# A decoder block in fp32 on one core: the order of the first stage's loads, table loads and bank hand-over

## The chip, the cores and the metric

The kernel runs on one core of one Trainium2 chip. The metric is device time in microseconds (us) of that core for one execution. A core has TensorE (PE: matmuls, its weight loads shown as PEld), VectorE (DVE), ScalarE (ACT), GpSimd (POOL) and SyncE (SP), whose queue issues all of this kernel's transfers.

## The reference, cut to what matters

One layer, batch 1, 512 tokens (T), width 2048 (D), everything fp32. The vector c sets shift, scale and gate of both sub-layers (adaLN).

```python
c_act = jax.nn.silu(c)
mod = c_act @ w_ada[l] + b_ada[l]
sh1, sc1, gt1, sh2, sc2, gt2 = jnp.split(mod[:, None, :], N_MOD, axis=-1)
h = _rmsnorm(x, norm1_g[l]) * (1.0 + sc1) + sh1
p = h @ w_in[l]
y_rwkv = _rwkv7_mixer(p[..., :N_RWKV_COLS], ...)
y_pool = _pool_mixer(p[..., N_RWKV_COLS:], pool_w[l], pool_b[l], pool_scale[l])
mix = jnp.concatenate([y_rwkv, y_pool], axis=-1) @ w_out[l]
x = x + gt1 * mix
h = _rmsnorm(x, norm2_g[l]) * (1.0 + sc2) + sh2
x = x + gt2 * _conv_ffn(h, w_up[l], conv_w[l], conv_b[l], w_down[l])
return _rmsnorm(x, norm_f_g)
```

## The kernel before, in words

The block is kept transposed: 128 channels on the partitions, 512 tokens along the row; x is 16 tiles of 128x512 (k = 0 to 15), loaded two at a time. A product of fp32 matrices is made of three (`mm3`, lines 112 to 114): each operand is cut into a hi part (fp32r) and a lo part, and PE adds hi x hi, lo x hi and hi x lo in one bank. `split_weights` does that for weights: a load of 256 KB to `wraw` (4 buffers), a cast on ScalarE to `whi` (line 106, 3 buffers), a subtraction on VectorE to `wlo` (line 108, 3 buffers). A pair `whi`, `wlo` serves 4 x 3 products.

**The first stage** makes modulated activations and, with them, the first eight tiles of the input projection.

1. Constants are loaded: `vec`, `cmat`, then the tables `masks`, `mlev`, `lanei` and `prec` (lines 69 to 78), which only the mixer and the pool read.
2. c is loaded to every partition (`cb`, line 171, 1 MB) and put through Silu on ScalarE (line 172); its first row is stored to `cact` in DRAM, from where the mixer's later adaLN work reads it again as `cq`.
3. x is loaded. ScalarE squares its tiles (`sq`, two buffers, line 188), VectorE adds them up in `sacc` (line 189, 15 adds, each on the one before).
4. `rms_stats` sums over the partitions on PE (`pst`), `rms_rows` takes the root on ScalarE (line 152, with a load of the table of functions) and the reciprocal on VectorE, makes four diagonal tiles (`rdiag`, line 156), and `rms_bcast` multiplies them on PE by ones (`psb`), so that each partition holds the row of 1/rms. ScalarE copies it (`rs`, line 193).
5. The loop over k: two rows of `mod` come from two adaLN products on VectorE (line 204; a tile `wa` of 1 MB, 128x2048, against `cb`, with the sum along the row; parts 1 and 0 are scale and shift). Then `gsc` (line 206), the shift's bias (line 208), and `modulate`: `h` on VectorE (line 139), the hi part `ah` on ScalarE (line 140), the lo part `al` on VectorE (line 141). Two weight tiles of 512 columns are split, and 8 x 3 products go into the eight banks `pf[0]` to `pf[7]`.

**The joint.** All eight banks are read out. `shift` (lines 225 and 226) is a scaled copy on ScalarE and a shifted multiply-add on VectorE: `xwa`, `xg1`, `xg2` from the first three banks, with Tanh and two Sigmoids behind them, then r, k, v of the first pair of heads; the last two banks are copied to `upad` (line 257) for the pooling. Then the pool of banks `ps0` is closed, and `psa` takes the same banks for the mixer. Its first tile in the order of work is a projection tile `mm`, 48 products (16 k x 3).

**The second stage** is the mixer: `win_pair(p)` projects three tiles for pair p, shifts and stores them; `start_pair`, `stage_b` and `stage_c` are a pair's chain of decays, triangular inverses and states, with many short steps on PE, VectorE and ScalarE. `pool_front` and `pool_back` make one group of the pooling (windowed sums on VectorE, line 275; two by two products on PE, line 290). `ada_rest` spreads 192 further adaLN products (`jkr`, line 343, 128x512) over the pairs.

A scheduler sets the order on each engine from the order of the program and from priorities: what stands in `with hp():` goes ahead of other work that is ready. On an engine instructions then run in that order, each waiting for what it reads. SP issues the transfers one by one, in its order; a transfer also waits for the one eight before it. `reuse_waits` says what a tile of a new pool waits for: by default for all readers of the space that the pool takes over, with "tile" for those of the tile's own space.

```python
pool_back(3, pool_front(3), load_pw(3))
with hp():
    q = start_pair(0)
    stage_b(0, q)
win_pair(1)
for p in range(NP):
    if p + 1 < NP:
        if p + 2 < NP:
            win_pair(p + 2)
        with hp():
            qn = start_pair(p + 1)
```

Of the kernel before, what the change touches and what calls it, by code (L numbers as in the profile page):

```python
# [9 lines left out]
F32 = mybir.dt.float32  # L10
# [44 lines left out]
def block_kernel(ctx, tc, a, out, stop=None, dbg=None):  # L55
# [13 lines left out]
    nc.sync.dma_start(masks, a["mask4"][:, :, :])  # L69
    mlev = cp.tile([P, 2, 64], F32, tag="mlev", name="mlev")  # L70
    nc.sync.dma_start(mlev, a["mlev"][:, :, :])
# [4 lines left out]
    nc.sync.dma_start(lanei, a["lanei"][:, :, :])  # L76
    prec = cp.tile([P, 16], F32, tag="prec", name="prec")
    nc.sync.dma_start(prec, a["prec"][:, :])
# [90 lines left out]
    if True:  # L169
        cb = p0.tile([P, D], F32, tag="cb", name="cb")  # L170
        nc.sync.dma_start(cb, a["c"][0:1, :].partition_broadcast(P))
        S.activation(cb, cb, AF.Silu)
        nc.sync.dma_start(cact, cb[0:1, :])
        xs = []
        for i in range(8):
            xt = p0.tile([P, 2, T], F32, tag=f"x{i}", name=f"x{i}")
            nc.sync.dma_start(xt, a["xT"][:, 2 * i : 2 * i + 2, :])
            xs += [xt[:, 0, :], xt[:, 1, :]]
        rstd = p0.tile([P, T], F32, tag="rs0", name="rs0")
        with tc.tile_pool(name="ps00", bufs=1, space=PSUM) as ps00:  # L180
            pst = ps00.tile([P, NC], F32, tag="st", name="pst")
            acc = p0.tile([P, T], F32, tag="sacc", name="sacc")
            for k in range(KT):
                if k == 0:
                    S.activation(acc, xs[k], AF.Square)
                    continue
                sq = p0.tile([P, T], F32, tag="sq", name="sq", bufs=2)
                S.activation(sq, xs[k], AF.Square)
                V.tensor_add(acc, acc, sq)
            rms_stats(pst, acc)  # L190
            psb = ps00.tile([P, T], F32, tag="bc", name="psb")
            rms_bcast(psb, rms_rows(p0, pst, NC), NC)
            S.copy(rstd, psb)
# [4 lines left out]
        for k in range(KT):  # L198
            for part in (1, 0):
                j = part * 16 + k  # L200
                wa = p0.tile([P, D], F32, tag="wa", name="wa", bufs=4)
                nc.sync.dma_start(wa, a["ada1"][j, :, :])
                jk = p0.tile([P, D], BF16, tag="jk", name="jk", bufs=1)
                V.scalar_tensor_tensor(jk, wa, 1.0, cb, op0=ALU.mult, op1=ALU.mult,
                                       accum_out=mod[:, j : j + 1])
# [6 lines left out]
            H.append((hi, lo))  # L212
            for i0 in range(0, 8, WC // P):
                wh, wl = split_weights(a["win0"][k, :, i0 * P : i0 * P + WC])
                for ii in range(WC // P):
                    sl = slice(ii * P, (ii + 1) * P)
                    mm3(pf[i0 + ii], wh[:, sl], wl[:, sl], *H[k], start=k == 0, stop=k == KT - 1)
# [5 lines left out]
        if True:  # L223
            def shift(ps, m, dst):
                S.activation(dst, ps, AF.Copy, scale=drv[:, m : m + 1])
                V.scalar_tensor_tensor(dst[:, 1:T], ps[:, 0 : T - 1], col("mu", m), dst[:, 1:T],
                                       op0=ALU.mult, op1=ALU.add)
# [8 lines left out]
            shift(pf[0], 24, xwa)  # L236
            S.activation(xwa[0:64, :], xwa[0:64, :], AF.Tanh)
            xg1 = ra.tile([P, T], F32, tag="xg1", name="xg1")
            shift(pf[1], 25, xg1)
            S.activation(xg1, xg1, AF.Sigmoid)  # L240
            xg2 = ra.tile([P, T], F32, tag="xg2", name="xg2")
            shift(pf[2], 26, xg2)
            S.activation(xg2, xg2, AF.Sigmoid)
# [14 lines left out]
            ps0ctx.close()  # L258

# [40 lines left out]
    psa = psctx.enter_context(tc.tile_pool(name="psa", bufs=1, space=PSUM))  # L300
# [320 lines left out]
    pool_back(3, pool_front(3), load_pw(3))  # L621
    with hp():
        q = start_pair(0)
        stage_b(0, q)
    win_pair(1)
# [358 lines left out]
```

## Time and profile before

| | |
|---|---|
| three runs | 2449.73, 2451.7, 2455.32 us; median 2451.7 |
| profiled execution | 2452.14 us; span from the first to the last instruction 2450.0 us; mean granted clock of TensorE 0.992 |
| PE busy | 2347.1 us (96% of the span), 13714 products |
| VectorE busy | 1408.7 us (57%) |
| ScalarE busy | 874.6 us (36%) |
| GpSimd busy | 23.7 us (1%) |
| transfers | 352.61 MB, mean 144 GB/s |

How to read it: times in the rows are counted from the start of the span. Busy shares are means over stages that differ; the stretches of rows 1 below tell them apart. In a row of the timeline the first number is the start, the second the time from the first start to the last end, "x8" says how many instructions stand together, and the bracket gives the idle time of the engine ahead of them and what ended it. The clock in a stretch is the granted one, 1.00 being 2.4 GHz.

### The profile page before, as it was taken

Reading aid. Unit: us, or ns where it says so; the run is one execution under the profiler, and the core shown is the slowest. Engines: PE = TensorE matmul, PEld = TensorE weight load, DVE = VectorE, ACT = ScalarE, POOL = GpSimd, SP = SyncE. Lnnn points to the kernel's source line nnn. Section 1 sums busy time; section 2 is a strip of 40 time slices with the busy share of each in tenths; the row PEclk is TensorE's granted clock in tenths of the full one; section 3 lists DMA queues with packets and bytes.
Section 4 is the critical chain, followed back from the end, with each engine's and each line's share of the span. In section 5 each row is a group of like instructions: output and inputs, shape, how many; then the busy total and the mean of one; then the engine's idle time right before and its main releaser. Section 6 shows DMA issues by size and latency. Waiting matters only on the chain.

```text
span 2450.0 us, 36089 instructions
## 1 busy us (share of the span) xinstructions
PE 2347.1 (96%) x13714; PEld 1872.0 (76%) x13714; DVE 1408.7 (57%) x2698; ACT 874.6 (36%) x1402; POOL 23.7 (1%) x29
## 2 busy tenths in 40 slices
PE   4889999999999999999999999999999999999997
PEld 3656666667667889887888888888888888888887
DVE  7987677787774357757534443444344434444457
ACT  3244443443433336532223322333233323323333
POOL 0000000000000002100000000000000000000000
PEclk9999999999999999999999999999999999999999
DMA  9975564556662635538533333333332333332335
GB/s 353 337 233 152 166 185 140 163 162 178 169 200 85 203 111 185 181 113 260 161 96 98 96 98 95 99 96 98 95 99 95 99 95 99 95 99 95 99 97 174
DMA packets 232160, 352.61 MB, mean 144 GB/s; under 512 B 74865, under 2 KB 80177, under 8 KB 227761
## 3 DMA queue, kind: packets, MB, share of 16 engines
q1 hardware_dynamic: 231986, 350.30, 46.0%
q8 instruction: 107, 1.75, 0.3%
q14 instruction: 67, 0.55, 0.1%
HBM read 334.22 MB, written 16.00 MB: 143 GB/s over the span
## 4 chain that ended last, share of the span: by engine, by line
PE 68%; DMA 3%; DVE 2%; ACT 1%; issue 0%; SPq 0%; POOL 0%; DVEq 0%; ACTq 0%; POOLq 0%
PE b L112 20%; PE b L114 20%; PE b L113 20%; DMA wraw<-wup 1%; PE mm L112 1%; PE mm L113 1%; PE mm L114 1%; DMA war<-ada 0%; PE pa L290 0%; DMA slot<-ada 0%; DMA wraw<-wdn 0%; DVE wlo L108 0%; DVE x L863 0%; PE pa L114 0%; PE pa L113 0%
## 5 line engine op out<-in xcount | busy, mean ns | idle before, releaser
L108 DVE TENSOR_TENSOR wlo<-wraw,whi 128x512 fp32r<-128x512 f32 x772 | 533.2, 692 | 694.9 <-ACT whi L106 679.6
L106 ACT CAST whi<-wraw 128x512 fp32r<-128x512 f32 x788 | 489.3, 622 | 1229.0 <-PE b L113 925.2
L114 PE MATMUL b<-hh,wlo 128*128 128x512 f32 (+1 forms) x1472 | 561.2, 381 | 5.9 <-DVE wlo L108 5.0
L112 PE MATMUL b<-hh,whi 128*128 128x512 f32 (+1 forms) x1472 | 560.0, 380 | 0.0
L113 PE MATMUL b<-hl,whi 128*128 128x512 f32 (+1 forms) x1472 | 559.5, 380 | 0.0
L112 PE MATMUL b<-ah,whi 128*128 128x512 f32 (+1 forms) x992 | 353.4, 357 | 4.3 <-ACT whi L106 2.5
L114 PE MATMUL b<-ah,wlo 128*128 128x512 f32 (+1 forms) x992 | 351.9, 355 | 0.8 <-DVE wlo L108 0.8
L113 PE MATMUL b<-al,whi 128*128 128x512 f32 (+1 forms) x992 | 352.1, 355 | 0.0
L114 PEld LDWEIGHTS b<-hh,wlo 128*128 128x128 f32 x1472 | 277.0, 188 | 62.1 <-DVE wlo L108 8.5
L112 PEld LDWEIGHTS b<-hh,whi 128*128 128x128 f32 x1472 | 276.9, 188 | 52.9 <-ACT whi L106 0.5
L113 PEld LDWEIGHTS b<-hl,whi 128*128 128x128 f32 x1472 | 277.0, 188 | 52.3
L112 PEld LDWEIGHTS b<-ah,whi 128*128 128x128 f32 x992 | 187.5, 189 | 33.7 <-ACT whi L106 4.3
L113 PEld LDWEIGHTS b<-al,whi 128*128 128x128 f32 x992 | 187.6, 189 | 27.4 <-DVE al L134 1.1
L114 PEld LDWEIGHTS b<-ah,wlo 128*128 128x128 f32 x992 | 187.6, 189 | 26.8 <-DVE wlo L108 1.2
L112 PE MATMUL mm<-ah,whi 128*128 128x512 f32 x464 | 192.4, 415 | 6.3 <-ACT upad L257 5.5
L113 PE MATMUL mm<-al,whi 128*128 128x512 f32 x464 | 191.8, 413 | 0.0
L114 PE MATMUL mm<-ah,wlo 128*128 128x512 f32 x464 | 190.1, 410 | 0.0
L343 DVE SCALAR_TENSOR_TENSOR jkr<-war,cq 128x512 bf16<-128x512 f32 x192 | 131.3, 684 | 18.7 <-DMA war<-ada 15.9
L848 DVE SCALAR_TENSOR_TENSOR x<-b,mod,x 128x512 f32<-128x512 f32 x80 | 59.7, 750 | 111.4 <-PE b L114 111.3
L112 PEld LDWEIGHTS mm<-ah,whi 128*128 128x128 f32 x464 | 88.4, 190 | 35.1 <-issue 10.4
L113 PEld LDWEIGHTS mm<-al,whi 128*128 128x128 f32 x464 | 88.3, 190 | 29.3 <-issue 13.0
L114 PEld LDWEIGHTS mm<-ah,wlo 128*128 128x128 f32 x464 | 88.4, 191 | 23.8 <-issue 6.3
(259 smaller groups left out, 2282.0 us busy)
## 6 DMA issues: line engine op xcount, KB each, us to landing
wraw<-wup SPq DMA_DIRECT2D x368, 256.0 KB, 3.0
war<-ada SPq DMA_DIRECT2D x192, 256.0 KB, 3.4
wraw<-wdn SPq DMA_DIRECT2D x192, 256.0 KB, 2.7
wraw<-win SPq DMA_DIRECT2D x140, 256.0 KB, 4.0
wa<-ada SPq DMA_DIRECT2D x32, 1024.0 KB, 6.9
wraw<-wout SPq DMA_DIRECT2D x88, 256.0 KB, 3.0
slot<-ada SPq DMA_DIRECT2D x64, 256.0 KB, 3.7
sp<-spill SPq DMA_DIRECT2D x21, 256.0 KB, 2.7
```

The costliest lines, as they stand in the source:

```text
L106: S.copy(hi, raw)
L108: eng.tensor_tensor(lo, raw, hi[:, :].bitcast(F32), op=ALU.subtract)
L112: PE.matmul(ps, wh, xh, start=start, stop=False)
L113: PE.matmul(ps, wh, xl, start=False, stop=False)
L114: return PE.matmul(ps, wl, xh, start=False, stop=stop)
L343: V.scalar_tensor_tensor(jk, wa, 1.0, cq[0], op0=ALU.mult, op1=ALU.mult, accum_out=modq[:, kq, j : j + 1])
L848: V.scalar_tensor_tensor(x2[f], ps, mod[:, 80 + f : 81 + f], x2[f], op0=ALU.mult, op1=ALU.add)
```

## The change

It has these parts:

- The loads of the four tables leave the constants' place and stand in the loop at k = 8, behind `modulate`.
- Two adaLN tiles (k = 0, scale and shift) are loaded ahead of x and multiplied ahead of the squares; the loop makes no adaLN product at k = 0.
- A root of one column (`warm`) stands in the program behind Silu.
- The store of `cact` moves behind the loads of x. The squares have four buffers instead of two.
- Tanh and the Sigmoids stand behind all six shifts and both copies. The pool `psa` has `reuse_waits="tile"`.
- The projection of pair 1 stands ahead of the pool's last group and of pair 0 in the program, and that group is inside `hp()`.

The diff, cut to its core:

```diff
@@ constants
-    nc.sync.dma_start(masks, a["mask4"][:, :, :])
-    nc.sync.dma_start(mlev, a["mlev"][:, :, :])
-    nc.sync.dma_start(lanei, a["lanei"][:, :, :])
-    nc.sync.dma_start(prec, a["prec"][:, :])
+    def load_tables():
+        nc.sync.dma_start(masks, a["mask4"][:, :, :])
+        nc.sync.dma_start(mlev, a["mlev"][:, :, :])
+        nc.sync.dma_start(lanei, a["lanei"][:, :, :])
+        nc.sync.dma_start(prec, a["prec"][:, :])
@@ first stage
+        def load_ada(k, part):
+            wa = p0.tile([P, D], F32, tag="wa", name="wa", bufs=4)
+            nc.sync.dma_start(wa, a["ada1"][part * 16 + k, :, :])
+            return wa
+
+        def ada(k, part, wa):
+            j = part * 16 + k
+            jk = p0.tile([P, D], BF16, tag="jk", name="jk", bufs=1)
+            V.scalar_tensor_tensor(jk, wa, 1.0, cb, op0=ALU.mult, op1=ALU.mult, accum_out=mod[:, j : j + 1])
+
         cb = p0.tile([P, D], F32, tag="cb", name="cb")
         nc.sync.dma_start(cb, a["c"][0:1, :].partition_broadcast(P))
         S.activation(cb, cb, AF.Silu)
-        nc.sync.dma_start(cact, cb[0:1, :])
+        warm = p0.tile([P, 1], F32, tag="warm", name="warm")
+        S.activation(warm, eps[:, 0:1], AF.Sqrt)
+        early = [load_ada(0, 1), load_ada(0, 0)]
+        ada(0, 1, early[0])
+        ada(0, 0, early[1])
...
+        nc.sync.dma_start(cact, cb[0:1, :])
...
-                sq = p0.tile([P, T], F32, tag="sq", name="sq", bufs=2)
+                sq = p0.tile([P, T], F32, tag="sq", name="sq", bufs=4)
...
         for k in range(KT):
-            for part in (1, 0):
-                j = part * 16 + k
-                wa = p0.tile([P, D], F32, tag="wa", name="wa", bufs=4)
-                nc.sync.dma_start(wa, a["ada1"][j, :, :])
-                jk = p0.tile([P, D], BF16, tag="jk", name="jk", bufs=1)
-                V.scalar_tensor_tensor(jk, wa, 1.0, cb, op0=ALU.mult, op1=ALU.mult,
-                                       accum_out=mod[:, j : j + 1])
+            if k:
+                for part in (1, 0):
+                    ada(k, part, load_ada(k, part))
...
             H.append((hi, lo))
+            if k == 8:
+                load_tables()
@@ out of the banks
-            shift(pf[0], 24, xwa)
-            S.activation(xwa[0:64, :], xwa[0:64, :], AF.Tanh)
...
-            shift(pf[1], 25, xg1)
-            S.activation(xg1, xg1, AF.Sigmoid)
...
-            shift(pf[2], 26, xg2)
-            S.activation(xg2, xg2, AF.Sigmoid)
+            for i, t in enumerate((xwa, xg1, xg2)):
+                shift(pf[i], 24 + i, t)
...
             ps0ctx.close()
+            S.activation(xwa[0:64, :], xwa[0:64, :], AF.Tanh)
+            S.activation(xg1, xg1, AF.Sigmoid)
+            S.activation(xg2, xg2, AF.Sigmoid)
...
-    psa = psctx.enter_context(tc.tile_pool(name="psa", bufs=1, space=PSUM))
+    psa = psctx.enter_context(tc.tile_pool(name="psa", bufs=1, space=PSUM, reuse_waits="tile"))
@@ second stage
-    pool_back(3, pool_front(3), load_pw(3))
+    win_pair(1)
     with hp():
+        pool_back(3, pool_front(3), load_pw(3))
         q = start_pair(0)
         stage_b(0, q)
-    win_pair(1)
```

The order in three places. The names carry numbers of buffers where a name has several.

**VectorE, from the start to the first `h`**, before:

```order
L100 TENSOR_SCALAR b1p<-vec 128x16
L189 TENSOR_TENSOR sacc<-sacc,sq 128x512 x15
L204 SCALAR_TENSOR_TENSOR jk,mod<-wa,cb 128x2048
L153 RECIPROCAL rstd<-rstd 128x4
L206 SCALAR_TENSOR_TENSOR gsc_88<-mod,b1p,vec 128x1
L156 TENSOR_SCALAR rdiag<-cmat,rstd 128x128 x4
L204 SCALAR_TENSOR_TENSOR jk,mod<-wa,cb 128x2048
L108 TENSOR_TENSOR wlo<-wraw,whi 128x512
L208 TENSOR_TENSOR mod<-mod,vec 128x1
L108 TENSOR_TENSOR wlo<-wraw,whi 128x512
L139 SCALAR_TENSOR_TENSOR h<-x_118,gsc_88,rs_134 128x512
```

and now:

```order
L102 TENSOR_SCALAR b1p<-vec 128x16
L180 SCALAR_TENSOR_TENSOR jk,mod<-wa,cb 128x2048
L221 SCALAR_TENSOR_TENSOR gsc_84<-mod,b1p,vec 128x1
L180 SCALAR_TENSOR_TENSOR jk,mod<-wa,cb 128x2048
L223 TENSOR_TENSOR mod<-mod,vec 128x1
L208 TENSOR_TENSOR sacc<-sacc,sq 128x512 x15
L155 RECIPROCAL rstd<-rstd 128x4
L158 TENSOR_SCALAR rdiag<-cmat,rstd 128x128 x4
L110 TENSOR_TENSOR wlo<-wraw,whi 128x512 x2
L141 SCALAR_TENSOR_TENSOR h<-x_123,gsc_84,rs_140 128x512
```

The two adaLN products (`jk`) have gone from behind the sums and from between `rdiag` and the weight split to ahead of all sums, with what follows them (`gsc`, the addition to `mod`).

**ScalarE, from the last squares to the root**, with the semaphores that each waits for, before:

```order
L188 ACTIVATE sq<-x_130 128x512 [waits DMAHW6_49,DVE_49]
L188 ACTIVATE sq<-x_130 128x512 [waits DVE_49]
L188 ACTIVATE sq<-x_132 128x512 [waits DMAHW7_49,DVE_49]
L188 ACTIVATE sq<-x_132 128x512 [waits DVE_49]
L152 ACT_TABLE_LOAD [waits PE_49]
L152 ACTIVATE rstd<-pst,eps 128x4 [waits Pool_49]
```

and now, first the beginning and then the same place:

```order
L188 ACT_TABLE_LOAD
L188 ACTIVATE warm<-eps 128x1 [waits Pool_49]
L185 ACT_TABLE_LOAD
L185 ACTIVATE cb<-cb 128x2048 [waits DMAHW2_49]
L204 ACTIVATE sacc<-x_123 128x512 [waits DMAHW5_49]
```

```order
L207 ACTIVATE sq<-x_135 128x512 [waits DMAHW3_49,DVE_49]
L207 ACTIVATE sq<-x_135 128x512 [waits DVE_49]
L207 ACTIVATE sq<-x_137 128x512 [waits DMAHW4_49,DVE_49]
L207 ACTIVATE sq<-x_137 128x512 [waits DVE_49]
L154 ACT_TABLE_LOAD
L154 ACTIVATE rstd<-pst,eps 128x4 [waits PE_49]
```

The new root `warm` has come out ahead of Silu, with a table load each, and a table load stands ahead of the root of the sums as before. The wait for PE has moved from that load to the root behind it.

**The joint, on ScalarE**, from the third shift to the weight casts, before:

```order
L225 ACTIVATE xg_1057<-pf_207,drv 128x512
L237 ACT_TABLE_LOAD
L237 ACTIVATE xwa<-xwa 64x512
L240 ACT_TABLE_LOAD
L240 ACTIVATE xg_1053<-xg_1053 128x512
L243 ACTIVATE xg_1057<-xg_1057 128x512
L225 ACTIVATE rkv<-pf_208,drv 128x512
L225 ACTIVATE rkv<-pf_209,drv 128x512
L225 ACTIVATE v<-pf_210,drv 128x512
L257 COPY upad<-pf_211 128x512
L257 COPY upad<-pf_212 128x512
L106 CAST whi<-wraw 128x512 x6
```

and now:

```order
L242 ACTIVATE xg_1053<-pf_213,drv 128x512
L242 ACTIVATE rkv<-pf_214,drv 128x512
L242 ACTIVATE rkv<-pf_215,drv 128x512
L242 ACTIVATE v<-pf_216,drv 128x512
L270 COPY upad<-pf_217 128x512
L272 ACT_TABLE_LOAD
L272 ACTIVATE xwa<-xwa 64x512
L270 COPY upad<-pf_218 128x512
L273 ACT_TABLE_LOAD
L273 ACTIVATE xg_1052<-xg_1052 128x512
L274 ACTIVATE xg_1053<-xg_1053 128x512
L108 CAST whi<-wraw 128x512 x5
```

**The joint, on VectorE**, from the last shift on, before:

```order
L226 SCALAR_TENSOR_TENSOR v<-pf_210,vec,v 128x511
L275 TENSOR_TENSOR sw<-upad 128x527
L108 TENSOR_TENSOR wlo<-wraw,whi 128x512
L275 TENSOR_TENSOR sw<-sw 128x525
L108 TENSOR_TENSOR wlo<-wraw,whi 128x512
L275 TENSOR_TENSOR sw<-sw 128x521
L343 SCALAR_TENSOR_TENSOR jkr,modq<-war,cq 128x512
L275 TENSOR_TENSOR sw<-sw 128x513
```

and now:

```order
L243 SCALAR_TENSOR_TENSOR v<-pf_216,vec,v 128x511
L269 MEMSET upad 128x16 x2
L291 TENSOR_TENSOR sw<-upad 128x527
L291 TENSOR_TENSOR sw<-sw 128x525
L291 TENSOR_TENSOR sw<-sw 128x521
L291 TENSOR_TENSOR sw<-sw 128x513
L359 SCALAR_TENSOR_TENSOR jkr,modq<-war,cq 128x512
L296 SCALAR_TENSOR_TENSOR z<-sw,upad 128x512
L291 TENSOR_TENSOR sw<-upad 128x527
L297 TENSOR_TENSOR z<-sw,prec 128x16
L110 TENSOR_TENSOR wlo<-wraw,whi 128x512
```

On ScalarE the functions and their table loads have moved behind the six shifts (Tanh stands ahead of the second copy, not behind it), and the casts stand behind all of them in both; on VectorE the first weight split (`wlo`) has moved from behind one sum of the pool to behind five, an adaLN product (`jkr`) and the first two `z`.

## Rows read from the trace of the kernel before

**Rows 1.** Stretches: start:end us, length; busy us (count); PEclk; DMA share; GB/s

```profile
0.00:10.00 10.00, 0.00 (x0) 0.00 (x0) 0.41 (x4) 1.28 (x1) 0.90 (x9) 1.00 0.77 260
10.00:14.00 4.00, 0.00 (x0) 0.00 (x0) 0.44 (x1) 3.42 (x4) 0.00 (x0) 1.00 1.01 384
30.00:150.00 120.00, 94.95 (x362) 72.10 (x362) 115.78 (x160) 30.04 (x49) 0.00 (x0) 0.96 0.88 319
161.00:166.50 5.50, 5.07 (x12) 4.03 (x13) 5.50 (x12) 1.35 (x3) 0.00 (x0) 0.50 0.53 179
200.00:700.00 500.00, 483.73 (x4655) 333.25 (x4655) 378.83 (x1010) 212.54 (x323) 0.00 (x0) 1.00 0.58 168
```

**Rows 2.** Waits of VectorE, 30 to 150 us: us in total, times, longest

```profile
DVE al L141 <- ACT ah L140: 2.5, 13, 0.2
DVE wlo L108 <- ACT whi L106: 0.7, 1, 0.7
```

**Rows 3.** Timeline of VectorE, the sums to the first modulate

```profile
19.59 6.26 DVE L189 TENSOR_TENSOR sacc<-sacc,sq 128x512 f32<-128x512 f32 x8 [0.55 <-ACT sq L188]
25.77 2.29 DVE L204 SCALAR_TENSOR_TENSOR jk<-wa,cb 128x2048 bf16<-128x2048 f32 x1
...
33.94 0.74 DVE L139 SCALAR_TENSOR_TENSOR h<-x,gsc,rs 128x512 f32<-128x512 f32 x1
```

**Rows 4.** Timeline of PE at the joint

```profile
155.56 0.39 PE L114 MATMUL pf<-ah,wlo 128*128 128x512 f32 x1
161.44 0.76 PE L112 MATMUL mm<-ah,whi 128*128 128x512 f32 x1 [5.48 <-ACT upad L257]
...
166.60 0.39 PE L112 MATMUL mm<-ah,whi 128*128 128x512 f32 x1
...
175.08 1.10 PE L290 MATMUL pa<-z,pw 128*128 128x512 f32 x2
```

**Rows 5.** Timeline of SP's queue, the first issues

```profile
1.66 0.42 SPq L69 DMA_DIRECT2D masks<-mask  x1
...
3.85 0.43 SPq L171 DMA_DIRECT2D cb<-c  x1
```

**Rows 6.** Transfers issued from 0 to 60 us: count, KB each, median us to landing

```profile
wa<-ada SPq DMA_DIRECT2D x12, 1024.0 KB, 7.4
...
cb<-c SPq DMA_DIRECT2D x1, 1024.0 KB, 6.7
cmat<-cmat SPq DMA_DIRECT2D x1, 320.0 KB, 3.3
vec<-vec SPq DMA_DIRECT2D x1, 297.5 KB, 3.0
```

**Rows 7.** Timeline of ScalarE, the norm's root and the copy of its rows

```profile
27.86 1.28 ACT L152 ACT_TABLE_LOAD   x1 [2.93 <-PE pst L147]
29.15 0.26 ACT L152 ACTIVATE rstd<-pst,eps 128x4 f32<-128x4 f32 x1
...
32.70 0.59 ACT L193 COPY rs<-psb 128x512 f32<-128x512 f32 x1 [2.26 <-PE psb L160]
```

**Rows 8.** Timeline of ScalarE, the hi part of an activation late in the loop

```profile
141.76 0.72 ACT L140 ACTIVATE ah<-h,mod 128x512 fp32r<-128x512 f32 x1 [1.88 <-DVE mod L208]
```

**Rows 9.** Timeline of ScalarE at the joint, first shift and first casts

```profile
152.36 0.69 ACT L225 ACTIVATE xwa<-pf,drv 128x512 f32<-128x512 f32 x1 [2.20 <-PE pf L114]
...
161.18 1.17 ACT L106 CAST whi<-wraw 128x512 fp32r<-128x512 f32 x2
```

**Rows 10.** The load of cq: SP's timeline, and the view of its tile

```profile
155.88 1.21 SPq L339 DMA_DIRECT2D cq<-cact  x1
...
DMA to landing us min/median/max: 5.2/5.2/5.2
```

**Rows 11.** Costliest groups: busy us, mean ns; idle before, releaser

```profile
L108 DVE TENSOR_TENSOR wlo<-wraw,whi 128x512 fp32r<-128x512 f32 x772 | 533.2, 692 | 694.9 <-ACT whi L106 679.6
...
L343 DVE SCALAR_TENSOR_TENSOR jkr<-war,cq 128x512 bf16<-128x512 f32 x192 | 131.3, 684 | 18.7 <-DMA war<-ada 15.9
```

**Rows 12.** Waits of PE, 160 to 1000 us: us in total, times, longest

```profile
PE pa L409 <- DVE bt L401: 4.1, 2, 2.2
```

## The prediction

> **What bounds the kernel now.** I read the stretches first. From 30 to 150 us VectorE (DVE) is busy 115.78 of 120 us and TensorE (PE) 94.95; from 200 to 700 us PE is busy 483.73 of 500 [rows 1]. So the first stage runs at VectorE's pace and what follows at PE's. The list of what VectorE waited for in that stage says that no transfer holds it: 2.5 us for the hi half of an activation, 0.7 us for a weight cast, no DMA [rows 2]. Whatever is saved ahead of the first modulate of k 0 (the instruction `h`, at 33.94 us [rows 3]) or at the joint between the stages reaches the end; what is saved on transfers does not, unless VectorE waits for them.
>
> The joint is the other place. PE's last product of the first stage starts at 155.56 and the next one at 161.44, 5.48 us idle, held by the copies of `upad` [rows 4]. Then it runs slow: between 161 and 166.5 us the granted clock is 0.50, 1.2 of 2.4 GHz, after that idle spell [rows 1]. Twelve products take 5.16 us, 0.43 each, and the 37 up to 175.08 take 0.229 each [rows 4].
>
> **Part 1: two adaLN tiles ahead of x.** The four tables leave the front of SP's queue: the load of `c` is issued 2.19 us earlier (3.85 less 1.66) [rows 5], with 0.40 MB less ahead of it. But the two tiles of 1,024 KB now stand before x [rows 6]. How long do they take? By 10 us 2.6 MB have moved, after that 0.384 MB a microsecond [rows 1]. When `c` landed (3.85 + 6.7 = 10.55 us [rows 5, 6]) the loads up to it made 2.08 MB, while 2.81 MB had moved: 0.73 MB belonged to later loads. Through the second tile it is 0.63 (`vec`, `cmat`) + 1.05 + 2.10 = 3.78 MB, so it lands between 13.1 us (nothing later moves along) and 15.0 us (0.73 MB does). I take 14.1, the middle. Its product with `c` takes 2.29 us and a short read of the sum [rows 3]: VectorE is free at 16.5 us. Then come the 15 adds of the squares at 0.78 us each (8 in 6.26 us [rows 3]), 11.7 us, to 28.2 us. Before, they ended at 25.85. Four buffers for the squares instead of two gain nothing: VectorE adds without a gap already. Nor is x late for them: its last tile closes 7.97 MB and lands at 25.9 us at the latest by the same rate, about 2 us before the end of the sums. So the sums end **2.35 us later** (1.35 to 3.25).
>
> **Part 2: from the sums to `h`.** Before, this takes 33.94 - 25.85 = 8.09 us, and two pieces of it go. ScalarE's table load for the square root begins at 27.86, when PE's sums are done, and the root follows at 29.15 [rows 7]. In the changed order it is still there, a third load, behind the new one and Silu's. But the wait for PE no longer sits on the load, it sits on the root behind it. So the load runs while PE works: **1.29 us** less. The Trainium skill (page "ScalarE: Activation LUTs", section "What ACT_TABLE_LOAD costs") gives a switch 1.28 us of load plus 1.38 us of drain. No drain shows here, the root starts 0.01 us behind the load; by the page the saving would be 2.66 us and the sum 1.4 us lower. The other piece: the broadcast rows are copied by 33.29 us [rows 7], and `h` started only at 33.94 because the second adaLN product and two weight splits stood in front of it. Now the product is done before and the splits fit in the wait: **0.65 us** less. `h` starts at 28.2 + 8.09 - 1.94 = 34.35 us, **0.4 us later** than before. Bounds: 33.35 (0.6 earlier, sums at 27.2) and 36.5 (2.6 later: sums at 29.1 and the load waiting as before).
>
> What becomes of the two products that were taken out of the loop? They cost nothing before: they filled VectorE's wait for PE and ScalarE between 25.77 and 32.7. Now VectorE idles there, since the next adaLN product stands behind `h` in its order.
>
> **Part 3: tables at k 8.** VectorE's order changes in one round: the lo half of activation 8 comes right behind the shift, without a weight split between. The hi half takes 0.72 us on ScalarE [rows 8] and today costs a wait of 0.2 [rows 2]: **0.6 us** more (0 to 1.3). The four loads take 2.19 us of SP's time ahead of the weight tiles of k 8. Those are fetched two rounds ahead, and VectorE never waited for a transfer here [rows 2]; I cost this at 0, with 2.2 us if that cover is gone.
>
> **Part 4: the joint.** PE's first projection tile now waits for the first bank alone, and goes on behind its last product at 155.8 us. Only the first 12 of its 48 products have their weights cast, and they are done at 155.8 + 12 x 0.229 = 158.5 us. The next cast stands in ScalarE's order behind all six shifts, both copies, two table loads and three functions, as before. That chain runs from 152.36 to 161.18 without a gap [rows 9], so the cast is done at 161.8. One thing is late next: in VectorE's order an adaLN product (`jkr`) now stands ahead of the next weight split, and its operand `cq`, issued at 155.88, lands 5.2 us later, at 161.1 [rows 10]. `jkr`, two sums of the pool and the split at 0.69 each [rows 11], overlapping by some 0.07, end at 163.75. PE, idle from 158.5 but for two products, goes on then. I keep the low clock as long behind the restart as before, 5.2 us, to 167.0: 7.6 products at 0.43, the rest at 0.229, and the 41 products that now precede the pool's are done at 171.45. Before, the 41st was done at 175.08 - 8 x 0.229 = 173.25. **Gain 1.8 us**, 3.3 if the clock stays full, 0 if the waits eat it.
>
> **The sum.** +0.4 + 0.6 + 0 - 1.8 = -0.8 us. The profiled execution took 2452.14 us (span 2450.0 and 2.14 around it), 0.44 above the median of 2451.7, so I forecast 2452.14 - 0.8 - 0.44 = **2450.9 us**. The rest of the mixer is reordered too, by the pool's work and the first pair moved behind the first projections. I cost that at nothing, since PE covers the pairs' chains for 97% of the time; what it may do is in the rivals.
>
> **The rivals.** *The pairs' chains come off PE's path* (0.21). For: the order puts the norm's product 7 projections behind the first pair's decay product instead of 17, so the chain that ends in `bt` starts its roots sooner; PE waited 4.1 us for `bt` in two pairs [rows 12]. If these go, and the clock stays full at the joint (1.5): 2450.9 - 5.6 = 2445.3 us. Against: two or three war loads and the same VectorE chain still stand between.
>
> *Less cover* (0.17), the slower side. Its place is the first product with `bt` in each pair: 43 projections stand between it and the decay product, 51 before, 8 x 0.229 = 1.8 us less to hide behind. PE was waiting there already [rows 12]. If the chain does not shorten and four of the eight pairs run so, 4 x 1.8 = 7.3 us: 2450.9 + 7.3 = 2458.2 us. It decides from three such pairs on. Against: PE's idle time between 200 and 700 us is 16 us in all [rows 1], so most pairs have room.
>
> *The load is not early* (0.12). The Trainium skill (page "ScalarE: Activation LUTs", section "Step-by-step: what each stage is for") says that the active tables hold one set of functions at a time. By that rule the new first load is lost, as the third load in the order says too, and only the place of the wait is left to gain by. If the third load runs at PE's end all the same, as its forerunner did [rows 7], 1.29 us come back: 2452.2 us, no change that can be measured.
>
> **How the numbers follow.** The forecast itself has 0.50; its own range is 2448 to 2454.5 (earliest `h` and full clock: 3.1 us less; latest sums, the load late or the joint without gain: 3.6 more). About 0.2% (4.9 us) is what a measurement of this kernel can tell from no change. Faster by more holds the first rival and a little of the forecast's tail: 0.23. Slower holds the second: 0.16. Within: 0.61, with the third rival. The range that leaves out two in ten runs from 2445, at the first rival, to 2457, just short of the second.
>
> **What would show it.** In the changed profile: the second adaLN product ends near 16.5 us, the adds near 28.2, the table load begins by 27, not behind PE, and `h` starts near 34.4. VectorE is idle some 4 us between. PE's joint shows two waits, near 158.5 for a cast and then for a weight split, and the pool's first product near 172 (its stage being 1 us later). The forecast is wrong if the adaLN tiles land after 15.5, if PE's joint shows no wait for the cast, or if PE's waits for `bt` total under 2 or over 8 us.

## The result and the profile after

Over 15 runs each, the changed kernel takes 2456.48 us in the median (2453.18 to 2460.81), the kernel before 2450.19 (2445.03 to 2455.84): ratio 1.0027, 95% interval 1.0019 to 1.0034. It is **6.3 us slower**, where 0.8 us faster was forecast. The profiled execution took 2459.8 us, with a span of 2458.1:

```profile
span 2458.1 us, 36089 instructions
...
PE 2354.1 (96%) x13714; PEld 1874.6 (76%) x13714; DVE 1409.5 (57%) x2698; ACT 875.2 (36%) x1404; POOL 24.0 (1%) x29
```

PE is busy 7 us longer than before with the same number of products. (The count is of records in the trace: most fp32 products of the mixer stand there as two.) That is the first sign of where to look: not a wait, but PE itself.

The start, in VectorE's timeline, answers to [rows 3]:

```profile
9.63 2.29 DVE L180 SCALAR_TENSOR_TENSOR jk<-wa,cb 128x2048 bf16<-128x2048 f32 x1 [5.43 <-DMA wa<-ada]
...
12.11 2.29 DVE L180 SCALAR_TENSOR_TENSOR jk<-wa,cb 128x2048 bf16<-128x2048 f32 x1
...
14.51 11.83 DVE L208 TENSOR_TENSOR sacc<-sacc,sq 128x512 f32<-128x512 f32 x15
...
32.47 0.75 DVE L141 SCALAR_TENSOR_TENSOR h<-x,gsc,rs 128x512 f32<-128x512 f32 x1 [1.58 <-ACT rs L212]
```

The second adaLN product starts at 12.11 us and `h` at 32.47, 1.5 us earlier than before. ScalarE's timeline, which answers to [rows 7], shows the table load ahead of the end of the sums and the root right behind PE:

```profile
23.84 1.28 ACT L154 ACT_TABLE_LOAD   x1
28.30 0.26 ACT L154 ACTIVATE rstd<-pst,eps 128x4 f32<-128x4 f32 x1 [3.18 <-PE pst L149]
```

VectorE's waits from 30 to 150 us, which answer to [rows 2]:

```profile
DVE al L143 <- ACT ah L142: 3.1, 13, 0.8
DVE h L141 <- ACT rs L212: 1.6, 1, 1.6
DVE wlo L110 <- ACT whi L108: 1.2, 1, 1.2
```

The longest wait for the hi half has grown from 0.2 to 0.8 us: that is k 8. The weight cast at k 1 makes VectorE wait 1.2 instead of 0.7. So of 1.5 us gained ahead of `h` in this execution, 0.2 is left where PE starts its last product of the stage (155.33 against 155.56).

The joint, in PE's timeline, answers to [rows 4]:

```profile
155.33 0.39 PE L116 MATMUL pf<-ah,wlo 128*128 128x512 f32 x1
155.56 0.39 PE L114 MATMUL mm<-ah,whi 128*128 128x512 f32 x1
...
161.62 0.50 PE L114 MATMUL mm<-ah,whi 128*128 128x512 f32 x1 [3.18 <-ACT whi L108]
161.95 0.40 PE L115 MATMUL mm<-al,whi 128*128 128x512 f32 x1
164.04 0.79 PE L116 MATMUL mm<-ah,wlo 128*128 128x512 f32 x1 [1.70 <-DVE wlo L110]
...
169.66 0.39 PE L114 MATMUL mm<-ah,whi 128*128 128x512 f32 x1
...
172.84 3.60 PE L306 MATMUL pa<-z,pw 128*128 128x512 f32 x8
```

PE goes on without a gap, stops for a cast, stops again for a weight split, and runs slow from 164.04 to 169.66 (13 products in 5.6 us). Its 41st product of the mixer, the last ahead of the pool's, starts at 172.60, where the 41st started at 172.97: 0.4 us ahead. The loss lies behind that. The busy time of PE's small products in the mixer, from the grouped view, first of the kernel before and then of the changed one:

```profile
L529 PE MATMUL pb<-ar,kt 64*128 64x256 f32 x128 | 32.4, 399 | 0.0
L527 PE MATMUL pb<-ar,bt 64*128 64x128 f32 x128 | 26.1, 322 | 0.0
L409 PE MATMUL pa<-ar,bt 64*128 64x128 f32 x128 | 12.0, 288 | 4.1 <-DVE bt L401 4.1
```

```profile
L545 PE MATMUL pb<-ar,kt 64*128 64x256 f32 x128 | 33.5, 402 | 0.0
L543 PE MATMUL pb<-ar,bt 64*128 64x128 f32 x128 | 28.0, 323 | 0.0
L425 PE MATMUL pa<-ar,bt 64*128 64x128 f32 x128 | 17.0, 301 | 3.5 <-DVE bt L417 3.5
```

The same 128 records of the pairs' decay products (`pa<-ar,bt`; 64 is the number of rows that the product sums over, half of PE's) occupy PE for 17.0 us instead of 12.0. PE's timeline says why. Before, the 16 of a pair stand together:

```profile
517.61 1.16 PE L409 MATMUL pa<-ar,bt 64*128 64x128 f32 x16
518.71 0.34 PE L539 MATMUL ch<-tok,L 128*64 128x64 f32 x4
```

In the changed kernel some of them stand between other products, those of 128 rows:

```profile
511.36 0.49 PE L425 MATMUL pa<-ar,bt 64*128 64x128 f32 x4
511.78 0.34 PE L555 MATMUL ch<-tok,L 128*64 128x64 f32 x4
...
512.26 0.48 PE L425 MATMUL pa<-ar,bt 64*128 64x128 f32 x2
512.68 0.34 PE L555 MATMUL ch<-tok,L 128*64 128x64 f32 x4
512.94 0.48 PE L425 MATMUL pa<-ar,bt 64*128 64x128 f32 x2
```

Sixteen in a row take 1.10 us, 0.14 for two; two alone take 0.42 until the next product. I call each such piece a stay at 64 rows. Four in a piece (511.36 to 511.78) take 0.42 too. The eight products of a pair are those of two heads, one on the lower 64 rows and one on the upper; in a piece of four or sixteen the records of the two heads start 6 to 7 ns apart in the trace and run side by side, in a piece of two (512.26 and 512.48) one head's product runs alone. So part of the 0.42 is the lost partner. Theory A: the new order of the mixer has more stays, and PE pays for each. The order listings bear it out: PE changes between products of 64 rows and 128 columns (`pa<-ar,bt`, `pb<-ar,bt`, `pb<-ar,kt`, `pa<-xwa,lw`) and all others 176 times before and 208 times now, and the decay products lie in 26 pieces instead of 14.

### The profile page after: what moved, and what is told of

Its sections match the earlier page's. It is cut to its first block, busy times and chain, and to the rows that moved or that the text cites. A ratio compares the mean times of both kernels' runs of the same rounds, so it can differ in the third digit from the quotient of the medians.

```text
span 2458.1 us, 36089 instructions
## 1 busy us (share of the span) xinstructions
PE 2354.1 (96%) x13714; PEld 1874.6 (76%) x13714; DVE 1409.5 (57%) x2698; ACT 875.2 (36%) x1404; POOL 24.0 (1%) x29
## 4 chain that ended last, share of the span: by engine, by line
PE 81%; DVE 8%; DMA 5%; ACT 3%; issue 2%; SPq 0%; POOL 0%; DVEq 0%; ACTq 0%; POOLq 0%
PE b L114 20%; PE b L116 20%; PE b L115 20%; PE mm L114 3%; PE mm L116 3%; PE mm L115 3%; DVE jk L180 3%; PE pb L545 1%; DVE wlo L110 1%; PE pb L543 1%; DMA wraw<-wup 1%; DMA x<-dxz 1%; PE pb L536 1%; DMA war<-ada 1%; PE pa L306 1%
## 5 line engine op out<-in xcount | busy, mean ns | idle before, releaser
L116 PEld LDWEIGHTS mm<-ah,wlo 128*128 128x128 f32 x464 | 87.8, 189 | 28.4 <-issue 8.8
```

Source lines behind the costliest of these rows:

```text
L116: return PE.matmul(ps, wl, xh, start=False, stop=stop)
```

## The experiments

The rivals to theory A were B, that the hand-over of the banks costs (the stop-and-go at the joint and what follows), and C, the first stage. The parts can be put in one by one, and the order of the mixer's instructions tells at once which of them move it: the first stage's edits and `reuse_waits` don't, word for word; moving the functions does, and so does the mixer's program.

| kernel | order of the mixer | ratio to before, 95% interval | median, us |
|---|---|---|---|
| first | before's | 0.9999, 0.9989 to 1.0009 | 2451.52 |
| tile_only | before's | 1.0001, 0.9990 to 1.0011 | 2450.42 |
| keep_order | before's | 1.0002, 0.9993 to 1.0011 | 2449.69 |
| mixer_new | its own | 1.0017, 1.0004 to 1.0029 | 2452.27 |
| no_tile | the changed kernel's | 1.0020, 1.0009 to 1.0031 | 2454.28 |
| changed kernel | its own | 1.0027, 1.0019 to 1.0034 | 2456.48 |
| funcs_late | that of joint | 1.0055, 1.0036 to 1.0073 | 2461.07 |
| joint | its own | 1.0087, 1.0067 to 1.0108 | 2470.04 |
| mixer_old | that of joint | 1.0090, 1.0073 to 1.0107 | 2471.10 |

**One part alone: first, joint, mixer_new.** `first` keeps the mixer's program, the functions between the shifts and the old wait; `joint` has only `reuse_waits` and the functions behind the shifts,

```diff
-            S.activation(xwa[0:64, :], xwa[0:64, :], AF.Tanh)
...
             ps0ctx.close()
+            S.activation(xwa[0:64, :], xwa[0:64, :], AF.Tanh)
```

and so for the two Sigmoids; `mixer_new` has only this:

```diff
-    pool_back(3, pool_front(3), load_pw(3))
+    win_pair(1)
     with hp():
+        pool_back(3, pool_front(3), load_pw(3))
         q = start_pair(0)
         stage_b(0, q)
-    win_pair(1)
```

> The kernel before with the first stage's part of the change alone (early adaLN tiles, tables at k 8, warm root, four buffers for the squares); the joint, the pool of banks and the mixer's program as before. The order of the mixer's instructions on every engine is then that of before: 176 changes on PE between products with 64 rows of weights and others, the products of the decay matrix (pa<-ar,bt) in 14 pieces. Theory A (the loss is in the mixer's new order: the pairs' small products are cut into more pieces, each change costs about 0.28 us of PE): 0.2 us faster than before, which is what the changed kernel's first stage gained. Theory B (the loss comes from the hand-over of the banks: the stop at the joint, the low clock behind it and what follows from it): the same, 0.2 us faster. Theory C (the loss comes from the first stage, whose transfers and tables lie elsewhere): 6 us slower than before.

> The kernel before with the joint's part alone (functions behind the shifts, a tile of the mixer's banks waits for its own bank only). The scheduler answers with another order in the mixer: 202 changes on PE between products of 64 rows and others instead of 176, the decay products in 21 pieces instead of 14. Theory A: 13 more stays times 0.28 us = 3.6 us more, less the 0.4 us that the joint gained in the changed kernel: 3.2 us slower than before. Theory B: all of it, 6 us slower. Theory C: no change but the joint's gain, 0.4 us faster.

> The kernel before with the mixer's part alone (first projection of pair 1 ahead, the pool's last group inside the high priority). 184 changes between products of 64 rows and others, the decay products in 17 pieces. Theory A: 4 more stays, 1.1 us slower than before. Theory B and C: no change.

`first` is at the time before: theory C falls. `mixer_new` is 0.17% slower, 4.2 us where A gave 1.1; the interval (1.0 to 7.1 us) just takes A in. In its profile the products of 64 rows take only 1.2 us more than in the order of before, so what the rest is, isn't shown. `joint` costs 21 us, far more than either A or B gave, and more than the whole change: the mixer's part takes most of it back. So the parts don't add up, as orders wouldn't.

**The hand-over and the order apart: no_tile, funcs_late, tile_only, mixer_old.** In the first, from the changed kernel:

```diff
-    psa = psctx.enter_context(tc.tile_pool(name="psa", bufs=1, space=PSUM, reuse_waits="tile"))
+    psa = psctx.enter_context(tc.tile_pool(name="psa", bufs=1, space=PSUM))
```

`funcs_late` is `joint` with that edit, `tile_only` is the kernel before with the reverse of it, and `mixer_old` is the changed kernel with the mixer's program of before.

> The changed kernel, but the mixer's first tile waits for all eight banks again. The order of the instructions on every engine is that of the changed kernel, word for word; only the waits differ. Theory A, as the runs so far have changed it (the time is set by which order the scheduler gives the mixer's instructions, not only by the number of pieces): 0.5 us slower than the changed kernel at most, 0.3% slower than before. Theory B (the hand-over of the banks costs what it is): back at the time before, ratio 1.000.

> The kernel before with Tanh and the Sigmoids behind the shifts, and nothing else; the mixer's first tile waits for all banks as before. The order on every engine is then word for word that of the joint's part alone, which took 21 us more than before. Theory A: that order is what costs, so 20 us slower than before (ratio 1.008). Theory B: as before, ratio 1.000.

> The kernel before with the hand-over alone: the mixer's first tile waits for its own bank only, and the order on every engine is that of before, word for word. Theory A: the joint's gain and nothing else, 0.5 to 1.5 us faster than before. Theory B: 6 us or more slower.

> The changed kernel with the mixer's program as before (the first projection of pair 1 behind pair 0's start). The mixer's order is then that of the joint's part alone. Theory A: as slow as that, some 20 us slower than before (ratio 1.008), so the mixer's part of the change takes back most of what the joint's part costs. Theory B: as the changed kernel, 6 us slower than before. If the profile of the joint's part owed its time to one long stretch at the low clock by chance, this second profile of the same order does not show that stretch.

B falls as the cause of the changed kernel's loss: without the hand-over it is still 0.20% slower than before, and the hand-over in the order of before changes nothing (1.0001). There the first tile's bank is still held by a shift that stands behind the functions: PE waits 4.7 us for it, where it waited 5.48.

In the order of `joint` the hand-over seems to matter: 1.0087 and 1.0090 with it, 1.0055 without, though the intervals touch. Both profiles with it show PE idle, 1.97 and 1.58 us, at 440 us, ahead of the norm's product `pa<-sq,cmat`, and then half the clock for 41 and 38 us. PE's timeline and stretches of `joint`, the latter with columns as in [rows 1]:

```profile
439.79 1.13 PE L390 MATMUL pa<-sq,cmat 128*128 128x512 f32 x2 [1.97 <-ACT sq L388]
...
430.00:435.00 5.00, 5.00 (x151) 3.77 (x145) 4.83 (x9) 1.94 (x3) 0.00 (x0) 1.00 0.59 179
440.00:445.00 5.00, 5.00 (x46) 3.97 (x46) 2.96 (x6) 4.79 (x6) 0.00 (x0) 0.59 0.23 61
...
460.00:465.00 5.00, 5.00 (x34) 3.10 (x35) 1.30 (x3) 0.27 (x1) 0.00 (x0) 0.50 0.51 157
475.00:480.00 5.00, 5.00 (x30) 2.51 (x27) 2.63 (x7) 0.49 (x2) 0.00 (x0) 0.50 0.54 116
485.00:490.00 5.00, 5.00 (x35) 3.06 (x36) 3.82 (x16) 0.85 (x2) 0.00 (x0) 1.00 0.44 122
```

In the profile of `funcs_late`, the same order, there is no such idle time and the clock is 1.00 from 430 to 485 us. But this spell isn't what makes the order slow. The two profiled executions are the slowest of their six (2483.30 and 2481.27 us), with mean clocks of 0.981 and 0.984; the other ten have 0.987 to 0.991, and 41 us at half the clock take 0.008 off the mean. So most of the others had no such spell, and took 2466 to 2474 us all the same. What the order of `joint` costs them, and whether the hand-over brings the spell on, stays open, and so does why the clock stays low that long while PE is busy.

**All but the new order: keep_order.** The changed kernel with the functions between the shifts and the mixer's program of before; everything else of the change is in.

> The changed kernel without the two edits that reorder the mixer (Tanh and the Sigmoids stand between the shifts as before, and the mixer's program is that of before); the early adaLN tiles, the late tables, the warm root and the hand-over of single banks are all in. The mixer's order is that of before, word for word. Theory A: at the time before, within 0.1% (the first stage's 1.4 us more against the joint's gain of at most 1.5), so 6 us faster than the changed kernel. Theory B or C: as slow as the changed kernel, ratio 1.003.

It is at the time before. The 6 us go with the two edits that reorder the mixer.

**Fewer stays: run16 and grouped16.** `run16` is the changed kernel with

```diff
-        for c in range(NC):
-            for h in range(2):
+        with tc.high_priority(offset=300000):
+            for c in range(NC):
+                for h in range(2):
```

around the decay products; `grouped16` is the kernel before with that, and in `stage_c` the products of `bt` and `kt` moved ahead of the three transposes, in a priority of the same kind:

```diff
-            pst = btile()
-            for i, src in enumerate((v, bt, kt)):
-                PE.transpose(pst[:, i * P : (i + 1) * P], src[:, cl], ident)
...
             pss = [btile() for h in range(2)]
...
+            pst = btile()
+            for i, src in enumerate((v, bt, kt)):
+                PE.transpose(pst[:, i * P : (i + 1) * P], src[:, cl], ident)
```

> The changed kernel with one more edit: the decay products of a pair have a still higher priority, so that they stand in one piece (8 pieces instead of 26, 178 changes of row count instead of 208); the rest of the order stays close to that of the changed kernel. Theory A: 15 stays less, 4.2 us faster than the changed kernel, so 2 us slower than before. Theory B and C: as the changed kernel, 6 us slower than before.

> The kernel before, with fewer changes of row count: the decay products of a pair in one piece, and in each chunk the products of bt and kt with ar ahead of the three transposes and of higher priority. PE stays 94 times at 64 rows instead of 118. Theory A by its price alone: 24 times 0.28 us = 6.7 us faster than before (ratio 0.997). Against that stands what the run with the decay products in one piece showed: a new order brings waits and spells of low clock of its own, which no count of pieces tells; with those, up to 6 us slower.

Both miss. `run16` takes 2461.3 us (1.0051, 1.0034 to 1.0068), slower than the changed kernel, at least in the median; `grouped16` 2454.12 (1.0011, 1.0001 to 1.0022). PE's time in products of 64 rows did come down in `run16`, from 120.7 us in the changed kernel (mean of four profiles, below) to 115.5. But the mean clock over its runs is 0.9894, against 0.9919 in the changed kernel; 0.0025 of 2450 us is 6 us, an estimate that takes all of PE's time to go with the clock. In `grouped16` PE has 71 stays in the trace, against 88 in the kernel before (half of 176), and yet its products of 64 rows take 115.2 us, no less than before (115.0). What has grown is the number of lost partners: 248 of its records of 64 rows and 128 columns start with no other within 20 ns, against 190 before, 190 in `run16` and 244 in the changed kernel. So the count of stays alone prices not even PE's own work, and it does not rank orders.

**The price of a stay: cut64 and cut128.** The kernel before with the decay products in one piece and 56 extra small products between them, seven a pair. The two kernels differ in one line, and their order in nothing (`-` is `cut64`, `+` is `cut128`):

```diff
-                    PE.matmul(pss[h][:, c * P : c * P + 64], bt[HS[h], nx], ar[HS[h], n // 2, 0, 0:64], start=True, stop=True)
+                    PE.matmul(pss[h][:, c * P : c * P + 64], bt[:, nx], ar[:, n // 2, 0, 0:64], start=True, stop=True)
```

> One half of a pair of kernels that measure the price of a change of row count. The kernel before, with the eight decay products of a pair in one piece, and between them seven extra small products of the same 64 rows (128x64 out, written where the next decay product writes over them), 56 in all. The order of all instructions is the same, word for word, as in its partner, whose extra products read 128 rows. Theory A: the 56 small products add themselves alone, some 0.05 us each, 3 us; with what the new order of the pairs brings besides, 0 to 12 us over the time before. Theory B: the same, since no bank is handed over otherwise.

> The other half: the same 56 extra products, the same order, but each reads all 128 rows, so PE changes its row count twice at each. Theory A: 56 times 0.28 us = 16 us slower than its partner with 64 rows (10 to 20). If changes of row count cost nothing, and pieces are a sign of something else: within 2 us of its partner.

`cut64` takes 2466.16 us (1.0073), `cut128` 2537.47 (1.0354): 71 us apart, over four times what was expected. The timeline of PE in `cut64`:

```profile
196.65 0.39 PE L413 MATMUL pa<-ar,bt 64*128 64x128 f32 x2
196.76 0.33 PE L412 MATMUL pa<-ar,bt 64*128 64x64 f32 x2
196.88 0.38 PE L413 MATMUL pa<-ar,bt 64*128 64x128 f32 x2
```

and in `cut128`, where the extra products read all rows:

```profile
197.24 0.43 PE L412 MATMUL pa<-ar,bt 128*128 128x64 f32 x2
197.61 0.49 PE L413 MATMUL pa<-ar,bt 64*128 64x128 f32 x2
198.02 0.43 PE L412 MATMUL pa<-ar,bt 128*128 128x64 f32 x2
198.39 0.71 PE L413 MATMUL pa<-ar,bt 64*128 64x128 f32 x2
```

From start to start it is 0.11 and 0.12 us in the first, 0.41 and 0.37 in the second: the way out of 64 rows costs 0.30, the way into them 0.25, 0.55 us a stay. I had priced one side only. 56 stays make 31 us. The rest goes with the clock, whose mean over the runs falls from 0.9897 to 0.9718; the last row shows it setting in, 0.71 for the same product. From 160 to 810 us, first `cut64`, then `cut128`:

```profile
160.00:810.00 650.00, 625.00 (x5662) 432.54 (x5663) 462.98 (x1194) 264.42 (x406) 0.00 (x0) 0.99 0.55 160
160.00:810.00 650.00, 626.04 (x5136) 424.41 (x5136) 430.66 (x1126) 236.55 (x358) 0.00 (x0) 0.90 0.52 149
```

The Trainium skill (page "TensorEngine Tiling (Array Packing)", section "Key Properties") says that changing the tiling mode drains TensorE. The trace agrees in that a change costs time, but the 0.25 to 0.30 us hold more than the change: in `cut64` neighbouring records start 0.05 to 0.07 us apart, in `cut128` each product of 64 rows runs alone, its two records 0.21 apart. The pair doesn't part the two. An estimate of the change itself comes from the sixteen at 517.61: inside the piece a pair of records is followed after 0.105 us, the last one by a product of another form after 0.20, so some 0.1 us a change.

**The split: three more profiles of the changed kernel.**

> The changed kernel once more, for its profile. If the pieces of 64 rows carry the loss, PE's time in the mixer without its waits and without the low clock is 700 us again (before: 688 to 693), and its products of 64 rows take 5 to 6 us more than before. If waits carry it, they come to 30 us or more (before: 24 to 27).

> The changed kernel once more, for its profile: as the run ahead of it.

> The changed kernel once more, for its profile: as the two runs ahead of it.

They took 2457.35, 2456.72 and 2455.05 us. I took PE's records from its last `pf` product to its first product in a bank `b`, which is the mixer and the first half of the output projection, and summed start to start by kind, with idle times of over 0.15 us counted as waits (in us; the products of 64 rows include those of 64 columns):

| | order of before, five profiles: mean (lowest to highest) | changed kernel, four: mean (lowest to highest) | difference |
|---|---|---|---|
| whole stretch | 723.7 (721.0 to 726.5) | 728.4 (727.8 to 729.0) | +4.7 |
| products of 64 rows | 114.7 (114.2 to 115.0) | 120.7 (120.5 to 120.8) | +6.0 |
| projections `mm` | 361.4 (358.9 to 363.2) | 363.0 (361.6 to 363.9) | +1.6 |
| other products | 223.0 (222.2 to 223.7) | 222.2 (221.9 to 222.5) | -0.8 |
| waits | 24.6 (22.8 to 25.9) | 22.5 (21.3 to 24.6) | -2.1 |

The five are before, first, tile_only, keep_order and fill. The products of 64 rows take more in every execution, with no overlap; the projections scatter by 4 us in one order, with the clock; the waits have not grown. A fifth profile of the changed order, that of `no_tile`, has 120.2 us in the products of 64 rows too, but only 723.3 in the whole; it is the fastest of its eleven executions (2445.35). By the 0.55 us of the pair above, 16 more stays would have made 8.8 us; 6.0 is what they took. The first stage ends 1.2 us later on the mean: its last product starts at 155.26 in eight profiles with the first stage of before (153.40 to 156.45) and at 156.46 in nine with the changed one (154.87 to 158.28). 4.7 and 1.2 make 5.9 of the 6.3 us, but that they come so near is in part luck: `first` and `keep_order` have the changed first stage and are at the time before. What follows, from there to PE's last product, has the same order in both and scatters by 9 us from one execution to the next, whatever the kernel (1553.1 to 1562.6). So the traces show where PE's time has grown in the new order; no experiment gave that time back alone (in `run16` it went and the loss stayed).

**A part left over: fill.** keep_order with the first adaLN product of k 1 in VectorE's idle time ahead of `h`:

```diff
+            dg = rms_rows(p0, pst, NC)
+            rms_bcast(psb, dg, NC)
+            ada(1, 1, load_ada(1, 1))
```

> The kernel that keeps the mixer's order (at the time before), with one more edit: the first adaLN product of k 1 is loaded next behind x and stands in VectorE's order between the diagonal tiles and the first modulate, where VectorE is idle for about 3 us in the changed kernel. If that idle time was what the early tiles left unused: the loop over k ends 2.3 us earlier and the time is 2.3 us below before (ratio 0.9991). If the tile lands too late (after 29 us) the product delays the first modulate by as much as it saves: no change.

2452.26 us, 1.0015 (1.0004 to 1.0027): not faster. In its profile the product fills the gap as meant:

```profile
31.66 2.28 DVE L180 SCALAR_TENSOR_TENSOR jk<-wa,cb 128x2048 bf16<-128x2048 f32 x1
...
34.53 0.75 DVE L141 SCALAR_TENSOR_TENSOR h<-x,gsc,rs 128x512 f32<-128x512 f32 x1 [0.58 <-ACT rs L214]
```

and the last lo half starts at 150.71 us, 0.9 ahead of `first`, whose tiles landed as late. But that execution is the fastest of its eleven runs (2445.53), so it doesn't show what slows the others; that stays open. No kernel of the study beats the one before.

## Why the prediction was wrong

**The step that failed** is the sentence under the sum: "The rest of the mixer is reordered too, by the pool's work and the first pair moved behind the first projections. I cost that at nothing, since PE covers the pairs' chains for 97% of the time". The experiments put the whole loss there: without the two edits that reorder the mixer the time is that of before (1.0002). The sentence asked only whether PE would wait. PE is the bound there, and a new order of its own instructions changes how long they take: +6.0 us in the products of 64 rows, which is more than the whole loss in the mixer (4.7), while the waits did not grow. Both pieces of evidence were at hand: the order listing (26 pieces instead of 14), and a trace of before in which sixteen in one piece took 1.10 us (at 517.61) and two apart 0.41 (at 658.23). It also put the reordering down to the pool's work and the first pair alone: moving the functions, taken as an affair of the joint, reorders the mixer too. None of the three signs that were to show the forecast wrong came, and all three asked about waits or landings. That the measured time lies below 2457 is luck: that bound was set just short of a rival that did not happen.

**Part 1 held in half of the executions.** In five profiles with the early tiles the second one lands at 14.1 to 14.4 us (14.1 forecast) and the sums end between 28.4 and 28.7, where 28.2 was forecast. In five others, the profile of the result among them, it lands at 12.0 to 12.4 and the sums end between 26.3 and 26.7, ahead of the bounds of 13.1 and 27.2. The forecast took over from before that 2.6 MB move by 10 us (260 GB/s); in the changed profile it is 326 GB/s.

**Part 2 held.** From the end of the sums to `h` it is 6.13 us (26.34 to 32.47); the sum gave 8.09 - 1.94 = 6.15. The table load runs early and no drain shows, so the 2.66 us of the Trainium skill (page "ScalarE: Activation LUTs", section "What ACT_TABLE_LOAD costs") would have been too much.

**Part 3 held**: 0.6 us for the hi half (3.1 against 2.5). The step left a further 0.5 out, the longer wait for a cast at k 1. Tables at k 8 brought no wait for a transfer.

**Part 4 was right in its course, and too large.** The stop for the cast came at 158.3 (158.5 forecast), the second for the split, PE went on at 164.04 (163.75). The gain came to some 0.1 us instead of 1.8: of the 0.37 us by which the 41st product is earlier, 0.23 stem from the first stage. The restart is 0.5 us later, counted from the stage's end. And the slow spell was counted from 161.8, with 7.6 products in what was left of it; at 161.62 the clock was still 1.00, it fell after that, and behind the restart 13 products ran slow, for 5.6 us. Against the whole, no gain of the hand-over can be measured.

**The rivals.** *The pairs' chains come off* and *less cover* both spoke of the wait for `bt`: it went from 4.1 to 3.5 us, two times as before, so neither happened. *Less cover* named a time near the result, 2458.2, by a mechanism that isn't there. *The load is not early* fell.

## What to carry to other kernels

Where a change makes a scheduler reorder the engine that is the bound, the order itself has a price: look in the new listing for products that were cut out of their pieces, and take what that costs from the trace before, where the same products stand together and apart. A count of the changes alone is not enough: it must tell which products lost the partner that they ran beside, and two orders with fewer changes (178 against 208 in `run16`, 142 against 176 in `grouped16`) were not faster than the kernels that they came from. Put parts that reorder and parts that only shift waits in separately; a comparison of orders, word for word, tells which is which before anything runs. A gain of a microsecond at one joint is no reason to accept a new order of the 700 us behind it.

## What the runs showed of the hardware that I had not expected

A change between products of 64 and of 128 rows costs PE 0.25 to 0.30 us in `cut128`, the loss of side-by-side running included. A product of 64 rows takes as long alone as two of them side by side on the two halves of PE's rows (0.42 us). The price isn't one of the row count alone: in the trace of before a `128*64` product of 64 columns is followed after 0.15 us by one of 64 rows (22 times) and after the same 0.15 by a `128*128` one (8 times), against 0.04 in the median by one of its own form. With 56 more stays the mean granted clock fell from 0.9897 to 0.9718, without more waiting (PE's waits in the stretch of the table: 28.9 and 28.2 us); which trait of those stays brings it down isn't shown. An idle time of 1.6 to 2.0 us at 440 us was followed by 38 to 41 us at half the clock, with PE busy all along, in two executions of one order. And the first adaLN tile lands either by 9.9 us or from 11.6 us on, in executions of the same program too (9.53 and 11.67), with nothing between in ten profiles.
